# Attention with TensorE's order written out in steps, one unit ahead, and an eighth softmax tile

## The chip, the cores and the metric

The kernel runs on one core of a Trainium2 chip. The core has five engines that work side by side and meet at semaphores: TensorE (PE in the profile; its weight loads have a row of their own, PEld), VectorE (DVE), ScalarE (ACT), GpSimd (POOL) and SyncE (SP), which here only issues DMAs. The metric is the device time of one execution in microseconds (us). The kernel before took 1780.21 us, the median of three runs from 1777.09 to 1782.11 us.

## What is computed

The reference is a two-layer diffusion backbone over 1024 latent tokens and 256 context tokens, model width 1024. Layer 0 is gated attention, layer 1 a bidirectional state-space mixer (Mamba-2), and a last normalisation follows. The change is in layer 0, whose core is:

```python
q = axial_rope(q, row, col); k = axial_rope(k, row, col)
def block(j):                                   # 128 queries
    qb = q[:, j*128 : j*128+128]
    kb = concat(k_pad[3 blocks around j], k_c)  # up to 3 x 128 latent keys and 256 context keys
    s = einsum('bqkgd,bskd->bkgqs', qb, kb) * scale
    p = softmax over the keys and one sink logit per head, with a band mask
    return einsum('bkgqs,bskd->bqkgd', p, vb)
y_lat = (o * silu(g)) @ w_out
```

There are 16 query heads in 4 groups of 4; each group shares one key and value head of width 64. Context queries see the context keys alone. The projections of q, k, v and the gate g come from one input product, and `w_out` projects the gated result back; a residual with a gate and the normalisation of layer 1 follow.

## The kernel before, in words

Every product of 32-bit data is made of three matmuls of a reduced-precision type: high by high, high by low and low by high parts (`mm3`, lines 238 to 240, written to a PSUM tile `pj`). The parts are made by a copy on ACT and a subtraction on DVE or POOL.

The tokens are cut in three pieces: piece 0 and 1 are the latent tokens 0 to 511 and 512 to 1023, piece 2 the 256 context tokens. Before the stage that the change touches, the keys, the values, and queries and gates of pieces 0 and 2 have been projected; queries and gate factors lie in DRAM. The stage, `attention`, then works through 40 **units**. A unit is one block of 128 queries with one group of four heads: 8 units of context queries (blocks 8 and 9), 16 of piece 0 (blocks 0 to 3), 16 of piece 1 (blocks 4 to 7). A unit has 2 key blocks for context queries, 4 for the blocks at the edges (0 and 7) and 5 for the others.

What a unit does, with the lines of the code before:

- **front** (`att_front`): POOL issues the loads of the queries `qs` (L748) and of their zero-padded other half `qz` (L753), SP the load of the gate factors `sgt` (L749). For each of four heads TensorE makes the scores into a PSUM tile `S` (L767 latent keys, L768 context keys, each twice, for high and low query parts). DVE adds mask and scale and takes the row minimum (L772), into a softmax tile `sm`; ACT takes the exponential and its row sum (L774). Then the sums get the sink's share and are inverted and spread out (`rs`, L777 to L782).
- **back** (`att_back`): for each key block TensorE transposes the four heads' probabilities into one PSUM tile `pt` (L793); ACT copies it to a high part `ph` (L797), DVE subtracts to get the low part `pl` (L798), and two matmuls add the products with the values to the PSUM tile `pv` (L799 with `ph`, L800 with `pl`). At the end `rs` is transposed (L806) and multiplied into the gate factors (L807); ACT copies half of `pv` (`co`, L809), two DVE additions join the halves (`ot`, L812), POOL multiplies by the gate (L813), and ACT and POOL split the result (L815, L816).

PSUM has eight banks: two `S` tiles of two banks, two `pt`, one `pv`, one `pj`.

In between run **projection parts**: the remaining input projections (gates and queries of piece 1) during the first 24 units, then the output projections of pieces 2 and 0 during the last 16. A projection of 512 tokens is cut in eight parts of three matmuls (piece 2 in four parts of six). How many parts have been issued is paced by the count of key blocks done (`tick`). When a projection ends, its `pj` bank is read out: a gate by ACT and DVE (L661, L662), a query by four DVE and POOL steps and a split (L621 to L624, L642, L643), an output by one DVE step (L859) that adds the residual.

The order of the instructions on each engine is not that of the code. A planner sorts them by priority and by its own estimate of when each is ready. Code can tie an instruction behind another one of the same engine (`issue_after`) and raise a priority (`high_priority`). Before the change only the projection parts are tied, each behind the value product of some blocks back (`PACE`); all other work of TensorE in this stage is placed by the planner, one unit of fronts ahead (`AHEAD = 1`).

Of the kernel before, what the change touches and what calls it, by code (L numbers as in the profile page):

```python
# [9 lines left out]
F32 = mybir.dt.float32  # L10
BF16 = mybir.dt.bfloat16
F32R = mybir.dt.float32r
# [5 lines left out]
P = 128  # L18
D = 1024
# [24 lines left out]
    rope_b=2, qf=3, qh=3, ql=2, kHH=2, kLL=2, qs=2, sgt=2, sm=7, mx=2, nm=2, es=2, sums=2, ph=2, pl=2, co=1, ot=2,  # L44
# [4 lines left out]
AHEAD = 1  # L49
PACE = 4  # L50
# [5 lines left out]
FIRST = 5  # L56
# [57 lines left out]
class Kernel:  # L114
# [251 lines left out]
    def rstd_n(self, pool, pn, n, width, size=512, rout=None, dout=None, scalar=False):  # L366

        nc, t, ps = self.nc, self.t, self.psA
# [10 lines left out]
        pr = t(ps, [P, 512], F32, self.ptag)  # L379
# [360 lines left out]
    def att_front(self, p, x, i, j, b):  # L740
        nc, t = self.nc, self.t
        ps = self.psA
        o = b * P - TT[i][0]
        sg = t(self.psm, [P, 2, P], F32, "sgt")
        nm = t(p, [P, R], F32, "nm")
        sums = t(p, [P, R], F32, "sums")
        qs = t(p, [P, R, P], F32R, "qs")
        nc.gpsimd.dma_start(qs, self.q_d[j][i][:, :, :, o : o + P].rearrange("e s d n -> (s d) e n"))  # L748
        nc.sync.dma_start(sg, self.sg_d[j][i][:, :, o : o + P].rearrange("e p n -> p e n"))  # L749

        z = j % 2
        qz = self.qz[z]
        nc.gpsimd.dma_start(qz[z * HD : (z + 1) * HD], self.q_d[j][i][:, z, :, o : o + P].rearrange("e d n -> d e n"))  # L753
        if b < 8:
            k0, k1 = max(b - 1, 0), min(b + 2, 8)
        else:
            k0, k1 = 8, 8
# [5 lines left out]
        for r in range(R):  # L763
# [5 lines left out]
            self.scored.append(scored.ins)  # L769
# [5 lines left out]
            sms.append(sm)  # L775
        es = t(p, [P, R], F32, "es")
# [6 lines left out]
        return j, b, i, o, kb, sms, sg, rs  # L783

    def att_back(self, p, st, oH, oL, tick):
        nc, t = self.nc, self.t
        ps = self.psA
        j, b, i, o, kb, sms, sg, rs = st
        pv = t(ps, [P, 512], F32, "pv")
        for x, bb in enumerate(kb):  # L790
            pt = t(ps, [P, R, P], F32, "pt")
            for r in range(R):
                nc.tensor.transpose(pt[:, r, :], sms[r][:, x * P : (x + 1) * P], self.ident)  # L793
            ph = t(self.pb, [P, R * P], F32R, "ph")
            pl = t(self.pb, [P, R * P], F32R, "pl")
            ptf = pt.rearrange("p r n -> p (r n)")
            nc.scalar.copy(ph, ptf)  # L797
            nc.vector.tensor_sub(pl, ptf, ph)  # L798
            nc.tensor.matmul(pv, self.v[:, bb, j, :], ph, start=x == 0, stop=False)  # L799
            mm = nc.tensor.matmul(pv, self.v[:, bb, j, :], pl, start=False, stop=x == len(kb) - 1)  # L800
            self.last.append(mm.ins)
            tick()

        pt = t(ps, [P, 512], F32, "pt")
        for e in range(2):
            nc.tensor.transpose(pt[:, e * P : (e + 1) * P], rs[:, e].rearrange("p x d -> p (x d)"), self.ident)  # L806
        nc.vector.tensor_mul(sg, sg, pt[:, : 2 * P].rearrange("p (a n) -> p a n", a=2))  # L807
        co = t(self.pb, [HD, 512], F32, "co")
        nc.scalar.copy(co, pv[HD:, :])  # L809
        ot = t(self.pb, [P, 2, P], F32, "ot")  # L810
        for e in range(2):
            nc.vector.tensor_add(ot[e * HD : (e + 1) * HD].rearrange("p a n -> p (a n)"), pv[:HD, e * 256 : (e + 1) * 256], co[:, e * 256 : (e + 1) * 256])  # L812
        nc.gpsimd.tensor_tensor(ot, ot, sg, op=ALU.mult)  # L813
        oh = oH[i][:, 2 * j : 2 * j + 2, o : o + P]
        nc.scalar.copy(oh, ot)  # L815
        nc.gpsimd.tensor_tensor(oL[i][:, 2 * j : 2 * j + 2, o : o + P], ot, oh, op=ALU.subtract)  # L816

    def attention(self, c0, ckv):
# [7 lines left out]
        t(p, [P, 384], F32, "pad")  # L826
# [16 lines left out]
        def out_steps(i):  # L843
# [25 lines left out]
            def norm():  # L869
                p = self.po  # L870
                rout = (p, [P, n], F32, "ut" if i == 2 else "sqa")
                st["r"] = self.rstd_c(p, st["acc"], n, D, rout=rout, dout=(p, [P, 512], F32, "dg0"))
                self.alloc_u(i)

# [8 lines left out]
            def fin():  # L883
                yield
                for f in steps:
                    f()

            steps = [norm] + [lambda k=k: mod(k) for k in range(KT)]
# [11 lines left out]
        self.last = []  # L900
        cur = nxt = None

        def tick(flush=False):

            seen[i] += 1
            while done[i] < (total[i] if flush else min(total[i], -(-total[i] * seen[i] // count[i]))):
                advance(i, self.last[max(-len(self.last), -PACE)])

        def advance(i, after):
            nonlocal cur, nxt  # L910
            with self.tc.high_priority(offset=-300), self.tc.issue_after(after):
                if cur is None:
                    cur = nxt or fill[i].pop(0)()
                    if nxt is None:
                        next(cur)
                    nxt = None
                    if fill[i]:
                        nxt = fill[i].pop(0)()
                        next(nxt)
                if next(cur, "end") == "end":  # L920
                    cur = None
            done[i] += 1
            if i == 1 and self.side and done[i] > KT * CPARTS and (done[i] - KT * CPARTS) % SIDE == 0:
                self.side.pop(0)()

        self.scored = []
        pend = [self.att_front(p, x, *units[x]) for x in range(AHEAD)]
        for x in range(FIRST):
            advance(2, self.scored[1 if x < FIRST // 2 else 3])
        for x, (i, j, b) in enumerate(units):  # L930
            if oH[i] is None:
                if i == 1:
                    i = 0
                    tick(True)
# [6 lines left out]
            if x + AHEAD < len(units):  # L941
                pend.append(self.att_front(p, x + AHEAD, *units[x + AHEAD]))
            self.att_back(p, pend.pop(0), oH, oL, tick)
        tick(True)
# [871 lines left out]
```

## Time and profile before

| what | value |
|---|---|
| median of three runs | 1780.21 us (1777.09 to 1782.11) |
| the profiled execution | 1780.27 us |
| its span, first to last instruction | 1778.4 us |
| PE busy, weight loads busy | 98%, 85% of the span |
| DVE, ACT, POOL busy | 68%, 49%, 45% |
| attention stage, by its first score and its last block | about 244 to 687 us |

A row of groups reads: line, engine, operation, the tiles written and read, shapes, count, then the busy time in us and the mean ns of one, then the idle time of the engine just before them and what ended it. A timeline row gives start and length of an instruction or of several merged. The end of a matmul is modelled and lies some 0.16 us after the time at which the next one can start, so the distance from start to start is what a matmul costs, and "98% busy" does not say that the array is never waiting.

### The profile page before, as it was taken

The numbers are of one execution on the slowest core, as the hardware profiler recorded it, in microseconds if no ns is written. First come the engines' busy times: TensorE is split into PE (matmuls) and PEld (weight loads), VectorE is DVE, ScalarE is ACT, GpSimd is POOL, SyncE is SP. The second block draws the span as 40 slices with busy tenths as digits, with TensorE's granted clock in tenths as the row PEclk, the third lists the DMA queues.
The fourth block names the chain that finished last, engine by engine and source line by source line (L and its number), as shares of the span: only waits on it lengthen the run. The fifth ranks groups of instructions, "written<-read, shape, count | busy, mean of one in ns | idle before, by whom it ended". The sixth has DMA issues, their size and how long they took to land.

```text
span 1778.4 us, 29177 instructions
## 1 busy us (share of the span) xinstructions
PE 1739.9 (98%) x10413; PEld 1505.5 (85%) x10413; DVE 1204.2 (68%) x2119; ACT 871.8 (49%) x1902; POOL 796.8 (45%) x1066
## 2 busy tenths in 40 slices
PE   9999999999999999999999999999999999999997
PEld 6897788888888787778898898989889898988887
DVE  5744446788877875684876867677685767876634
ACT  4522247777777774352444444344443434544522
POOL 3231047555565545103454553636455363554321
PEclk9999999999999999999999999999999999999998
DMA  9478855444455446222323233332333333655533
GB/s 361 169 216 256 293 145 143 101 103 106 113 151 132 117 109 217 74 64 63 81 73 91 81 81 84 83 82 72 92 81 76 89 81 80 180 165 168 182 102 117
DMA packets 211388, 225.53 MB, mean 127 GB/s; under 512 B 15788, under 2 KB 149036, under 8 KB 211244
## 3 DMA queue, kind: packets, MB, share of 16 engines
q1 hardware_dynamic: 177180, 205.02, 39.0%
q0 software_dynamic: 34064, 18.65, 5.7%
q8 instruction: 82, 1.34, 0.3%
q14 instruction: 62, 0.51, 0.1%
HBM read 188.78 MB, written 35.13 MB: 126 GB/s over the span
## 4 chain that ended last, share of the span: by engine, by line
PE 84%; DVE 8%; DMA 2%; ACT 2%; issue 2%; POOL 1%; SPq 0%; DVEq 0%; ACTq 0%; POOLq 0%
PE pj L1213 18%; PE pj L1247 10%; PE pj L1648 7%; PE pj L238 6%; PE pj L239 6%; PE pj L240 6%; PE psD L1198 4%; PE psX L1400 3%; PE pt L793 3%; PE psD L1316 2%; PE pv L800 2%; PE psX L1369 2%; PE psX L1368 2%; PE pv L799 2%; PE S L767 1%
## 5 line engine op out<-in xcount | busy, mean ns | idle before, releaser
L238 PE MATMUL pj<-uH,wh 128*128 128x512 f32 (+1 forms) x680 | 244.1, 359 | 3.9 <-DVE h L859 2.0
L240 PE MATMUL pj<-uH,wl 128*128 128x512 f32 (+1 forms) x680 | 230.1, 339 | 1.4 <-POOL wl L223 1.4
L239 PE MATMUL pj<-uL,wh 128*128 128x512 f32 (+1 forms) x680 | 230.5, 339 | 0.4 <-POOL uL L816 0.4
L1213 PE MATMUL pj<-uH,wh 128*128 128x512 f32 x512 | 173.8, 411 | 1.2 <-ACT bn L1168 1.2
L1213 PE MATMUL pj<-uH,wl 128*128 128x512 f32 x512 | 170.4, 403 | 0.0
L1213 PE MATMUL pj<-uL,wh 128*128 128x512 f32 x512 | 168.2, 403 | 0.0
L1291 POOL TENSOR_TENSOR xw<-xn,dtdec 128x256 f32<-128x256 f32 x144 | 95.5, 664 | 160.4 <-PE psD L1316 75.8
L238 PEld LDWEIGHTS pj<-uH,wh 128*128 128x128 f32 x680 | 129.3, 190 | 28.0 <-ACT wh L221 5.7
L1247 PE MATMUL pj<-wh,uH 128*128 128x256 f32 x512 | 150.7, 294 | 0.0
L1247 PE MATMUL pj<-wl,uH 128*128 128x256 f32 x512 | 150.5, 294 | 0.0
L1247 PE MATMUL pj<-wh,uL 128*128 128x256 f32 x512 | 150.2, 293 | 0.0
L798 DVE TENSOR_TENSOR pl<-pt,ph 128x512 fp32r<-128x512 f32 x168 | 114.0, 688 | 47.2 <-ACT ph L797 46.2
L240 PEld LDWEIGHTS pj<-uH,wl 128*128 128x128 f32 x680 | 128.8, 190 | 17.3 <-POOL wl L223 2.2
L239 PEld LDWEIGHTS pj<-uL,wh 128*128 128x128 f32 x680 | 129.7, 191 | 10.5 <-issue 1.1
L223 POOL TENSOR_TENSOR wl<-wr,wh 128x512 fp32r<-128x512 f32 x74 | 97.2, 1316 | 84.7 <-ACT wh L221 83.8
L772 DVE CUSTOM_DVE_ANT_0 sm<-S,mask,nsink 128x640 f32<-128x640 f32 (+2 forms) x160 | 119.2, 772 | 20.6 <-PE S L768 13.5
L1432 ACT ACTIVATE uT<-psX,nw 128x128 f32<-128x128 f32 x128 | 46.5, 363 | 171.7 <-PE psX L1431 167.7
L774 ACT ACTIVATE sm<-sm,nm 128x640 f32<-128x640 f32 (+2 forms) x160 | 118.7, 742 | 17.5 <-DVE nm L772 16.9
L797 ACT CAST ph<-pt 128x512 fp32r<-128x512 f32 x168 | 97.4, 585 | 56.7 <-PE pt L793 52.4
L221 ACT CAST wh<-wr 128x512 fp32r<-128x512 f32 (+1 forms) x116 | 74.5, 648 | 81.8 <-PE pj L239 58.4
L1213 PEld LDWEIGHTS pj<-uH,wl 128*128 128x128 f32 x512 | 96.0, 188 | 19.9
L1213 PEld LDWEIGHTS pj<-uL,wh 128*128 128x128 f32 x512 | 95.5, 188 | 19.2
(352 smaller groups left out, 4945.3 us busy)
## 6 DMA issues: line engine op xcount, KB each, us to landing
wr<-w_x SPq DMA_DIRECT2D x32, 512.0 KB, 4.2
M<-acs SPq DMA_DIRECT2D x64, 256.0 KB, 5.3
bw<-acs SPq DMA_DIRECT2D x64, 256.0 KB, 5.6
wr<-w_sk SPq DMA_DIRECT2D x24, 512.0 KB, 4.1
wr<-wg SPq DMA_DIRECT2D x40, 256.0 KB, 5.2
qs<-q POOLq DMA_DIRECT2D x40, 256.0 KB, 3.9
wada<-w_ada SPq DMA_DIRECT2D x16, 512.0 KB, 8.6
wr<-wq SPq DMA_DIRECT2D x32, 256.0 KB, 3.1
```

Source lines behind the costliest of these rows:

```text
L223: (eng or nc.vector).tensor_tensor(l, raw, h, op=ALU.subtract)
L238: self.nc.tensor.matmul(ps, lh, rh, start=first and i == 0, stop=False)
L239: self.nc.tensor.matmul(ps, lh, rl, start=False, stop=False)
L240: self.last_mm = self.nc.tensor.matmul(ps, ll, rh, start=False, stop=last and i == n - 1)
L772: nc.vector.tensor_tensor_reduce(out=sm[:, :W], in0=Sv, in1=self.mask[:, m0 : m0 + W], scale=-SCALE, scalar=self.nsink[:, 4 * j + r : 4 * ...
L774: nc.scalar.activation(sm[:, :W], sm[:, :W], AF.Exp, bias=nm[:, r : r + 1], scale=-1.0, accum_out=sums[:, r : r + 1])
L797: nc.scalar.copy(ph, ptf)
L798: nc.vector.tensor_sub(pl, ptf, ph)
L1213: self.pe = nc.tensor.matmul(raw[:, 512 * i : 512 * i + 512], l[:, k, :], r[i][:, k, :], start=k + y == 0, stop=k == KT - 1 and y == 2)
L1247: self.pe = nc.tensor.matmul(pj[:, c], l, r[:, k, :], start=c % 2 + q + k + y == 0, stop=c % 2 == 1 and q == 1 and k == 3 and y == 2)
L1291: nc.gpsimd.tensor_tensor(xw, X(st, c).rearrange("p (r h) -> p r h", r=R), self.dtdec[:, c, hd(d, g)].unsqueeze(2).broadcast_to([P, R, HP] ...
L1648: self.pe = nc.tensor.matmul(banks[x], l[:, z, sl], r, start=k == 2 * qs[0] and y == 0, stop=k == 2 * qs[-1] + 1 and y == 2)
```

## The change

`att_front` becomes a generator that yields after each head, and `att_load` issues its two query loads one unit earlier, right after the first head of the unit before. `att_back` is split into `att_turn` (the four transposes of one key block, ACT's copy, DVE's subtraction), `att_gate` (the transposes of `rs` and the multiplication) and `att_out`. A helper `tied` puts every group of TensorE's instructions in this stage behind the last one before it, so TensorE's order is that of the code:

- five heads are done before the first unit's products begin;
- then for key block k of a unit: the transposes of block k+1; projection parts that end a projection; one head of a later unit's scores (`HEADS_AT`); at k = 0 the rest of the parts; the product with `ph`; at k > 0 the rest of the parts; at the last block the transposes of the next unit's block 0; the product with `pl`; parts that begin a projection; at the last block but one the gate's transposes.

`PARTS_AT` says at which block a unit's parts are put. There are eight softmax tiles `sm` in place of seven; `rs` has one buffer in place of two, and an unused tile of 384 words (`pad`) is gone. The normalisation behind the output projection of piece 2 is cut in two steps (`norm`, `factor`) that are issued six parts apart.

```diff
-sm=7
+sm=8
-AHEAD = 1
-PACE = 4
-FIRST = 5
+PARTS_AT = {5: (0, 0, 1, 2, 3, 4), 4: (0, 0, 1, 2, 3), 2: (0, 0, 1, 0, 1)}
+HEADS_AT = {5: ((1, 0), (1, 0), (1, 0), (0, 0), (1, 0)), 4: ((1, 0), (1, 0), (1, 0), (1, 0)), 2: ((2, 1), (1, 0))}
...
-        rs = t(self.pb, [P, 2, 2, HD], F32, "rs", 2)
+        rs = t(self.pb, [P, 2, 2, HD], F32, "rs")
...
+    def att_turn(self, sms, x):
+        nc, t = self.nc, self.t
+        pt = t(self.psA, [P, R, P], F32, "pt")
+        for r in range(R):
+            mm = nc.tensor.transpose(pt[:, r, :], sms[r][:, x * P : (x + 1) * P], self.ident)
+        ph = t(self.pb, [P, R * P], F32R, "ph")
+        pl = t(self.pb, [P, R * P], F32R, "pl")
+        ptf = pt.rearrange("p r n -> p (r n)")
+        nc.scalar.copy(ph, ptf)
+        nc.vector.tensor_sub(pl, ptf, ph)
+        return mm, (ph, pl)
...
-        t(p, [P, 384], F32, "pad")
...
+        def tied(f, *args):
+            nonlocal last
+            with ExitStack() as c:
+                if last:
+                    c.enter_context(self.tc.issue_after(last.ins))
+                out = f(*args)
+            mm = out[0] if isinstance(out, tuple) else out
+            last = mm or last
+            return out
...
+        def stream():
+            q = [self.att_load(p, 0, *units[0])]
+            for x, u in enumerate(units):
+                for r, mm in enumerate(self.att_front(p, q[x], x, *u)):
+                    if r == 0 and x + 1 < len(units):
+                        q.append(self.att_load(p, x + 1, *units[x + 1]))
+                    yield mm
...
+            for k, bb in enumerate(kb):
+                if k + 1 < n:
+                    _, w1 = tied(self.att_turn, sms, k + 1)
+                ends = [edge(i, d + y) for y in range(want[k])]
+                d += want[k]
+                early = max([y + 1 for y in range(want[k]) if 1 in ends[y]], default=0)
+                late = want[k] - early if early or want[k] and 0 in ends[0] and k else 0
+                advance(i, early)
+                heads(HEADS_AT[n][k][0])
+                if k == 0:
+                    advance(i, want[0] - early - late)
+                    pv = t(ps, [P, 512], F32, "pv")
+                vv = self.v[:, bb, j, :]
+                tied(nc.tensor.matmul, pv, vv, w[0], k == 0, False)
+                heads(HEADS_AT[n][k][1])
+                if k:
+                    advance(i, want[k] - early - late)
+                if k == n - 1 and self.pend:
+                    _, w1 = tied(self.att_turn, self.pend[0][1], 0)
+                tied(nc.tensor.matmul, pv, vv, w[1], False, k == n - 1)
+                advance(i, late)
+                if k == n - 2:
+                    tied(self.att_gate, sg, rs)
+                w = w1
```

More of the change, by code (lines that the diff above doesn't have):

```diff
@@ L786, in att_back @@
         nc, t = self.nc, self.t
[L787 to L802, printed above, removed]
@@ L886, in fin @@
                     f()
-            steps = [norm] + [lambda k=k: mod(k) for k in range(KT)]
+                self.last_mm = None
+            steps = [norm, factor] + [lambda k=k: mod(k) for k in range(KT)]
             if i == 2:
@@ L926, in attention @@
[L926 to L929, printed above, removed]
+        cur = nxt = last = None
+        self.pend = []
+        def tied(f, *args):
[7 more added lines that the diff above has]
+            return out
@@ new lines, in part, with advance @@
+        def part():
+            nonlocal cur, nxt
+            self.last_mm = None
+            if cur is None:
+                cur = nxt or fill[i].pop(0)()
+                if nxt is None:
+                    next(cur)
+                nxt = None
+                if fill[i]:
+                    nxt = fill[i].pop(0)()
+                    next(nxt)
+            if next(cur, "end") == "end":
+                cur = None
+            return self.last_mm
+        def advance(i, m):
+            for _ in range(m):
+                with self.tc.high_priority(offset=-300):
+                    tied(part)
+                done[i] += 1
+                if i == 1 and self.side and done[i] > KT * CPARTS and (done[i] - KT * CPARTS) % SIDE == 0:
+                    tied(self.side.pop(0))
@@ new lines, in heads, with gate @@
+        def heads(m):
+            for _ in range(m):
+                if tied(next, scores, None) is None:
+                    break
+        def gate(x):
+            i, j, b = units[x]
+            o = b * P - TT[i][0]
+            sg = t(self.psm, [P, 2, P], F32, "sgt")
+            nc.sync.dma_start(sg, self.sg_d[j][i][:, :, o : o + P].rearrange("e p n -> p e n"))
+            return sg
+        scores = stream()
+        i = 2
+        for m, f in ((2, 2), (2, 2), (1, 1)):
+            heads(m)
+            advance(2, f)
```

96 lines of the change are left out of this document (52 added, 44 removed).

## The prediction

> **What bounds the kernel now.** I read the page first, then the busy time by stretches, then TensorE's groups with their shapes, the timeline, and last the waits of TensorE's weight loads.
>
> ```profile
> PE 84%; DVE 8%; DMA 2%; ACT 2%; issue 2%; POOL 1%; SPq 0%; DVEq 0%; ACTq 0%; POOLq 0%
> ```
>
> The chain that ended last is TensorE for 84%, so the question is how much of the attention stage TensorE spends on something other than issuing matmuls. The stretches are the stage (244 to 687 us) and ten of its five-block units; after the length stand the busy times of PE, PEld, DVE, ACT and POOL with their counts, the granted clock, and the DMA share.
>
> ```profile
> 244.00:687.00 443.00, 430.20 (x2517) 364.91 (x2515) 328.71 (x732) 314.46 (x719) 255.55 (x365) 1.00 0.50 124
> 371.04:491.18 120.14, 117.40 (x676) 99.20 (x675) 101.55 (x209) 84.97 (x183) 68.64 (x93) 1.00 0.47 108
> ```
>
> The clock is full (1.00). No other engine is full on the whole: DVE 328.71 of 443.00 us (74%), ACT 71%. In the ten units, where query projections are read out, DVE is at 85%. What a matmul costs is the distance between starts.
>
> ```profile
> 303.73 0.60 PE L793 MATMUL pt<-ident,sm 128*128 128x128 f32 x4
> 304.09 0.36 PE L767 MATMUL S<-kHH,qs 128*128 128x256 f32 x1
> 304.29 0.28 PE L768 MATMUL S<-kHH,qs 128*128 128x256 f32 x1
> 304.41 0.28 PE L767 MATMUL S<-kL,qz 128*128 128x256 f32 x1
> ...
> 405.35 0.40 PE L238 MATMUL pj<-uH,wh 128*128 128x512 f32 x1
> 405.58 0.39 PE L239 MATMUL pj<-uL,wh 128*128 128x512 f32 x1
> ...
> 406.04 0.34 PE L767 MATMUL S<-kHH,qs 128*128 128x384 f32 x1
> 406.22 0.28 PE L768 MATMUL S<-kHH,qs 128*128 128x256 f32 x1
> ```
>
> A 512-wide matmul costs 0.23 us (405.35 to 405.58), a 384-wide one 0.18, a 256-wide one 0.12 (304.29 to 304.41). Four transposes cost 0.36, and the matmul behind them 0.20 in place of 0.12: 0.44 together, 0.11 each.
>
> ```profile
> L793 PE MATMUL pt<-ident,sm 128*128 128x128 f32 x672 | 99.8, 273 | 0.1
> L238 PE MATMUL pj<-uH,wh 128*128 128x512 f32 x204 | 90.6, 444 | 1.3 <-DVE qf L662 0.9 <-DVE h L859 0.4
> L800 PE MATMUL pv<-pl,v 128*128 128x512 f32 x168 | 69.6, 414 | 6.1 <-DVE pl L798 5.4
> L768 PE MATMUL S<-kHH,qs 128*128 128x256 f32 x160 | 45.9, 290 | 0.3 <-DVE nm L772 0.3
> L767 PE MATMUL S<-kHH,qs 128*128 128x384 f32 x96 | 34.9, 363 | 0.1
> L238 PE MATMUL pj<-uH,wh 128*128 128x256 f32 x64 | 19.5, 305 | 1.6 <-DVE h L859 1.6
> L806 PE MATMUL pt<-ident,rs 128*128 128x128 f32 x80 | 15.3, 272 | 0.1
> L767 PE MATMUL S<-kHH,qs 128*128 128x256 f32 x32 | 10.2, 319 | 0.7 <-DVE nm L772 0.7
> ```
>
> L239 and L240 stand beside L238, L799 beside L800, the `kL,qz` half beside each `kHH,qs` row, with the same counts. So 3 x 204 + 2 x 168 = 948 matmuls of 0.23 (218 us), 2 x (160 + 32) + 3 x 64 = 576 of 0.12 (69), 192 of 0.18 (35), 672 + 80 transposes of 0.11 (83): 405 us. With some 8 us for the first matmuls of the next stage that fall into the window (an estimate, about 35 at 0.23), the floor is 413 of 443 us. About 30 us are waiting. The waits of the weight loads show the same sum, and where it lies:
>
> ```profile
> PEld pv L800 <- DVE pl L798: 13.8, 25, 2.3
> PEld pv L799 <- ACT ph L797: 3.7, 8, 1.1
> PEld pj L238 <- DVE h L859: 2.9, 3, 1.9
> PEld S L767 <- DVE nm L772: 2.1, 4, 0.8
> PEld pj L238 <- DVE qf L662: 1.3, 2, 1.1
> ```
>
> These make 23.8; nine smaller rows bring it to about 28. Products that wait for their split probabilities are 17.5 of that, the `pj` bank 4.2, scores 2.1.
>
> **The change, part by part.** It computes the same matmuls, so the floor stays; only the roughly 28 us can move, and what the new order adds. I compare, for each wait, the work that the order puts in between (the cover) with the chain that must fit behind it. The pieces from the costs above: a block's transposes 0.44, one head (two of 0.18, two of 0.12) 0.60, a part of three 0.69, a product 0.23, the gate's transposes 0.22. A five-block unit is then 5 x (0.44 + 0.46) + 4 x 0.60 + 5.8 parts (88 parts over 76 blocks) x 0.69 + 0.22 = 11.1 us, against 120.14 / 10 = 12.0 now.
>
> The chains, from these rows (the timeline around one unit's end, then groups of DVE in the ten units, of ACT at 288 to 462 us, and POOL's longest wait):
>
> ```profile
> 407.28 0.40 PE L800 MATMUL pv<-pl,v 128*128 128x512 f32 x1
> 407.52 0.60 PE L793 MATMUL pt<-ident,sm 128*128 128x128 f32 x4
> 407.72 0.58 ACT L809 COPY co<-pv 64x512 f32<-64x512 f32 x1 [0.58 <-PE pv L800]
> 409.19 0.84 DVE L812 TENSOR_TENSOR ot<-pv,co 64x256 f32<-64x256 f32 x2
> 410.28 0.40 PE L799 MATMUL pv<-ph,v 128*128 128x512 f32 x1
> 410.67 1.28 DVE L798 TENSOR_TENSOR pl<-pt,ph 128x512 fp32r<-128x512 f32 x2
> 411.41 0.50 PE L800 MATMUL pv<-pl,v 128*128 128x512 f32 x1 [0.73 <-DVE pl L798]
> ```
>
> ```profile
> L772 DVE CUSTOM_DVE_ANT_0 sm<-S,mask,nsink 128x640 f32<-128x640 f32 x41 | 34.9, 878 | 2.2 <-PE S L768 1.5 <-PE pt L793 0.6
> L798 DVE TENSOR_TENSOR pl<-pt,ph 128x512 fp32r<-128x512 f32 x50 | 34.0, 688 | 14.2 <-ACT ph L797 13.9
> L643 DVE TENSOR_TENSOR ql<-qf,qh 128x512 fp32r<-128x512 f32 x7 | 8.1, 1154 | 0.2
> L622 DVE STREAM_SHUFFLE rope_b<-pj 128x512 f32<-128x512 f32 x8 | 5.9, 738 | 0.0
> ```
>
> ```profile
> L774 ACT ACTIVATE sm<-sm,nm 128x640 f32<-128x640 f32 x43 | 35.6, 828 | 4.7 <-DVE nm L772 4.3
> ```
>
> ```profile
> POOL qs L748 <- PE S L768: 39.7, 24, 11.0
> ```
>
> - *Products.* From the last transpose to `pl`: about 0.4 until ACT starts (407.28 to 407.72 for the copy `co`), 0.58 for the copy as for `co`, 0.69: 1.7 us with both queues empty. With one exponential (0.83) and one mask step (0.88) in front it is 3.4; in the unit above it was 3.9 (407.52 to 411.41), behind four heads in a row. The new order puts a product, a part, a product, transposes, a head, a product and a part between: 0.23 + 0.69 + 0.23 + 0.44 + 0.60 + 0.23 + 0.69 = 3.1 us, and a step without a part or a head some 0.6 less. With one head a step there is seldom more than one exponential and one mask step in front, so most chains fit and some are late by a few tenths. Bounds for the sum: 0, and 24 (a third of 168 late by 0.4). I take 6, a third of today's 17.5, nearer the empty-queue row because the heads come singly.
> - *The bank `pv`.* The next unit's first product waits until `co` and both additions have read it: 0.4 + 0.58 + 0.84 = 1.9 with empty queues; above it took 2.75 (407.28 to 410.03). Cover: product 0.23, transposes 0.44, head 0.60, two parts 1.38, in all 2.65. Today the planner fills this place with whatever is ready; now nothing else may go first. Bounds 0 and 30 (`co` behind an exponential and the additions behind a mask step: 1.9 + 0.83 + 0.88 = 3.6, 0.95 late in 32 units of four or five blocks). I take 5, about 0.15 per unit, near the observed 2.75.
> - *The bank `pj`.* The part that ends a projection goes to the front of its step, the one that begins the next to the end of the following one: head 0.60, two products 0.46, transposes 0.44, head 0.60, two products: 2.5 us. A query needs 0.4, the shuffle's 0.74 and a multiplication of about its length, 1.9, plus its turn in DVE's queue. From 4.2 to 2; bounds 0 and 32 edges x 0.5 = 16.
> - *Scores and softmax tiles.* One head a step: both earlier readers of an `S` tile have two steps (over 4 us) for 0.88 and less. The eighth tile lets the head of the unit after next start when the last transposes are done. From 2.1 to 0.5; bounds 0 and 2. The rest (the nine smaller rows, 4.5, normalisation and gate among them) goes to 3, as the cut in `norm` and `factor` puts six parts between DVE's diagonal and its matmul.
> - *Queues passed.* The two query loads now come a unit ahead, right behind the last reader of their buffers, so POOL's 39.7 us of waiting at L748 should nearly go. POOL is off the chain, so I count nothing; it covers late low weights (L223). If it were not gone, weight splits behind it would hold L240. With one `rs` buffer POOL's copy must wait for the gate's transposes at the last block but one; the sums of the next unit are ready at about that time (its last head is at the third block, 3 us before), so at most some tenths, with the next loads and weight splits behind it. SP's gate load waits for a tile freed two units before, as now; the weight loads and output stores behind it wait the same.
>
> Sum of waits after: 6 + 5 + 2 + 0.5 + 3 = 16.5 us, against 28.3: 12 us less. The profiled execution took 1780.27, its span 1778.4, so 1.9 lie outside and stay; it agrees with the median 1780.21. Forecast: 1780.2 - 12 = **1768 us**.
>
> The Trainium skill (Perfetto Trace Analysis, Identifying the Most-Contended Engine) takes the weight loads' busy share, not the matmuls', as TensorE's headroom. Here that is 364.91 of 443.00, so 78 us of room and 1702 us; the distances between starts bear out 30, as a 512-wide matmul takes 0.23 whatever its load takes, so that time gets no chance.
>
> **The rivals.**
>
> 1. *Nearly all waits go.* The covers hold everywhere. 1780 - 26 = 1754. For it: empty-queue chains of 1.7 and 1.9 fit with room; against: DVE at 10.2 us per 11.1 us unit leaves queues seldom empty.
> 2. *DVE takes over as the limit; no change.* In the ten units DVE is busy 101.55 / 10 = 10.2 us per unit and waits 1.4 more for `ph` (13.9 / 10). If that wait stays, a unit cannot be under 11.6: 0.4 gained in each of 24 five-block units, 10 us, and late `pv` additions in the same queue give back 5 to 8. 1776. For it: the split L643 takes 1154 ns against 688 for L798 of the same size, so DVE is slowed there already. The Trainium skill (SBUF, Who interferes with whom) has a DVE instruction with two SBUF inputs, as L643, block whole against GpSimd's reads, while L798 has one input in PSUM; the two rows agree, and a denser unit would hit more of it: at another 0.5 us per unit DVE, not TensorE, sets the pace by an estimate from these rows.
> 3. *The single `pv` bank; slower.* ACT serves `co` behind an exponential and DVE the additions behind a mask step in every unit of four or five blocks: 0.95 x 32 = 30 us in place of 5, so 1768 + 25 = 1793. It decides from about (5 + 12 + 5) / 32 = 0.7 us late per unit. For it: fixed order, ACT at 71% and the new unit's `ph` due at the same moment; against: 2.75 observed with 2.65 of cover.
>
> **How the numbers follow.** My forecast, with its sum between 1760 and 1774, has 0.46; rival 1 0.18; rival 2 0.18; rival 3 0.18. The point is the likeliest case. Fast ends with rival 1 (1754), slow with rival 3 at nearly its full price, so 1752 to 1790; alone, my case has 1760 to 1774. A change under 0.3% (5 us) can't be told from none. Faster are my case and rival 1: 0.64; rival 2 the same: 0.18; rival 3 slower: 0.18.
>
> **What the changed profile would show.** Right: the stage near 431 us; L800's wait for `pl` under 6 us; POOL's wait at L748's counterpart almost gone; mask steps one at a time, not four in a row. Wrong: first products of a unit (`pv` with `ph`) waiting for the additions `ot` by more than 0.7 us each; first parts of a projection waiting for `pj`; DVE over 95% busy in the query units; or a transpose that waits for the exponential of the next unit's last head.

## The result, and the profile after

The changed kernel takes 1799.76 us (median of five runs, 1797.82 to 1807.75) against 1778.40 us of the kernel before beside it: a ratio of 1.0123, with a 95% interval from 1.0098 to 1.0149. It is slower by about 21 us; the forecast was 12 us faster. The profiled execution took 1797.82 us with a span of 1796.1.

The page of the changed kernel: TensorE's busy share and the chain that ended last.

```profile
PE 1736.1 (97%) x10413; PEld 1503.8 (84%) x10413; DVE 1197.3 (67%) x2119; ACT 877.8 (49%) x1902; POOL 793.5 (44%) x1066
...
PE 84%; DVE 7%; issue 3%; ACT 3%; DMA 2%; POOL 1%; SPq 0%; DVEq 0%; ACTq 0%; POOLq 0%
```

Same work, more waiting. The attention stage, which was forecast at 431 us, takes 450 (columns as in the prediction):

```profile
244.00:694.00 450.00, 414.31 (x2455) 352.77 (x2454) 321.16 (x728) 315.39 (x712) 247.89 (x360) 0.99 0.46 116
```

DVE is busy 321.16 of 450.00 us (71%) and ACT 70%: neither has become the limit. The waits of TensorE in that stretch say what has (L920 is the line of `tied` from which both products with the values now come, L237 to L239 are the projection's three matmuls, L810 is the gate's transpose, L798 a block's):

```profile
PE pv L920 <- DVE ot L820: 18.6, 17, 2.2
PE pj L237 <- DVE h L865: 4.0, 1, 4.0
PE pj L237 <- DVE qf L668: 3.6, 6, 0.9
PE pt L810 <- POOL rs L790: 3.0, 3, 1.5
PE pv L920 <- ACT wh L220: 1.4, 2, 0.9
PE pv L920 <- ACT ut L872: 1.2, 1, 1.2
PE S L775 <- DVE nm L778: 1.0, 2, 0.6
```

The first row is the bank of value sums: a unit's first product waits for the additions that read the last unit's sums. Before, the same view for the same stretch began:

```profile
PE pv L800 <- DVE pl L798: 5.4, 12, 1.9
PE pj L238 <- DVE h L859: 2.0, 2, 1.6
PE pv L799 <- DVE ot L812: 1.6, 2, 0.9
```

These idle times begin only when the modelled end of the last matmul is past, so they are too short. For the comparison of runs I took the distance from each start to the next within the stage, less the cost of the matmul by the prediction (0.23, 0.18, 0.12, 0.11 us), and summed what is over 0.15 us by the matmul that comes next. In us:

| kernel | unit's first product | low-part products | parts | gate | transposes | scores | all |
|---|---|---|---|---|---|---|---|
| before | 2.6 | 10.0 | 3.7 | 0.3 | 0.2 | 1.9 | 20.3 |
| after | 25.4 | 1.2 | 9.6 | 4.5 | 2.3 | 2.1 | 45.1 |

The column "all" also has 1.6 us before of places that are not listed. So the waits for `pl` are nearly gone, 8.8 us gained, and 22.8 us are lost at first products, 5.9 at the projection bank, 4.2 at the gate. The smaller losses per matmul, which the table leaves out, fell by some 4 us. One place of the bank's wait, from the timeline of the changed kernel:

```profile
377.05 0.83 ACT L780 ACTIVATE sm<-sm,nm 128x640 f32<-128x640 f32 x1 [2.06 <-DVE nm L778]
377.19 0.48 PE L920 MATMUL pv<-pl,v 128*128 128x512 f32 x1
377.51 0.60 PE L798 MATMUL pt<-ident,sm 128*128 128x128 f32 x4
377.88 0.56 ACT L802 CAST ph<-pt 128x512 fp32r<-128x512 f32 x1
378.47 0.58 ACT L817 COPY co<-pv 64x512 f32<-64x512 f32 x1
...
379.08 0.68 DVE L627 TENSOR_TENSOR qf<-pj,cos 128x512 f32<-128x512 f32 x1
379.69 0.73 DVE L628 STREAM_SHUFFLE rope_b<-pj 128x512 f32<-128x512 f32 x1
380.31 0.83 DVE L820 TENSOR_TENSOR ot<-pv,co 64x256 f32<-64x256 f32 x2
381.28 0.47 PE L920 MATMUL pv<-ph,v 128*128 128x512 f32 x1 [1.88 <-DVE ot L820]
```

The unit's last product starts at 377.19. With ACT free, the copy `co` could follow 0.4 us later. Here an exponential holds ACT until 377.88, and then ACT casts `ph`, the next unit's block 0, whose transposes the new order puts in front of that product. The copy ends at 379.05, but DVE reads out a query before it comes to the additions at 380.31, so at this place DVE's turn costs more than the cast. The next unit's first product starts 4.1 us after the last one, and TensorE stands for about 2 of them with scores, transposes and parts behind it that it may not issue. Over the 40 units the copy starts 1.23 us after the start of the last product on the mean, before 0.74. From 0.4 us after that product's start to the copy, ACT spends 20.1 us in all on the next unit's cast, before 0.4. The additions end at 3.09 us on the mean, before at 2.60: the whole difference, 0.49 us, arises ahead of the copy.

The stage also gives up some filling: the planner used to put matmuls of the next stage among the last units' waits, and mostly no longer does. The first of those into `S` tiles, before and after:

```profile
L238 PE MATMUL S<-uH,wh x40: 388/390/487, 670.7 to 722.7; 128*128 128x512 f32 x40
```

```profile
L237 PE MATMUL S<-uH,wh x40: 389/389/798, 693.4 to 739.0; 128*128 128x512 f32 x40
```

From its first score to its last product the stage takes 433.0 us before and 446.7 after, 13.7 more, though it holds some 7 us less work by the costs of the matmuls (397 in place of 404). That work comes later, and what follows the stage takes 4.8 us more; what precedes it takes 0.8 less. Together these are the 17.7 us between the two profiled spans.

Some long waits are followed by a lower clock. The granted clock is 0.50 in two short stretches of the changed kernel's stage (columns as before):

```profile
382.20:385.60 3.40, 3.40 (x14) 2.90 (x13) 2.56 (x4) 2.33 (x5) 1.99 (x3) 0.50 0.41 116
511.90:515.30 3.40, 3.40 (x16) 3.12 (x15) 0.87 (x2) 1.16 (x2) 0.09 (x1) 0.50 0.56 129
```

They begin 0.9 and 0.7 us after waits of 2.0 and 4.2 us have ended (at 381.28 and 511.22), and in the first one a 512-wide matmul takes 0.43 us to the next start (382.37 to 382.80) in place of 0.23. Other waits of 2.0 and 2.4 us, which end at 465.7 and 621.7, are followed by none. The kernel before has no such stretch in its stage. As an estimate, at most half of the 6.8 us is lost, 3.4 us; about 1.5 us of it stands in the table, among parts, scores, gate and transposes. The five executions of the changed kernel have a mean granted clock of 0.990 to 0.995, 0.992 on the mean, and the profiled one has 0.995; the kernel before has 0.992 to 0.998 in all the sessions below, 0.996 on the mean. By these means (0.004 of 1798 us) up to some 7 us of the 21 would be lost as clock, again an estimate. No run separates this share from the waits that it comes with.

### The profile page after: what moved, and what is told of

Read it like the earlier page. It is cut to its first block, busy times and chain, and to the rows that moved or that the text cites. A ratio compares the mean times of both kernels' runs of the same rounds, so it can differ in the third digit from the quotient of the medians.

```text
span 1796.1 us, 29272 instructions
## 1 busy us (share of the span) xinstructions
PE 1736.1 (97%) x10413; PEld 1503.8 (84%) x10413; DVE 1197.3 (67%) x2119; ACT 877.8 (49%) x1902; POOL 793.5 (44%) x1066
## 4 chain that ended last, share of the span: by engine, by line
PE 84%; DVE 7%; issue 3%; ACT 3%; DMA 2%; POOL 1%; SPq 0%; DVEq 0%; ACTq 0%; POOLq 0%
PE pj L1296 18%; PE pj L1330 10%; PE pj L1731 7%; PE pj L237 6%; PE pj L238 6%; PE pj L239 6%; PE psD L1281 4%; PE pv L920 4%; PE psX L1483 3%; PE pt L798 3%; PE psD L1399 2%; PE S L774 2%; PE psX L1452 2%; PE psX L1451 2%; PE S L775 1%
## 5 line engine op out<-in xcount | busy, mean ns | idle before, releaser
L237 PE MATMUL pj<-uH,wh 128*128 128x512 f32 (+1 forms) x680 | 235.9, 347 | 7.9 <-DVE h L865 4.0
L239 PE MATMUL pj<-uH,wl 128*128 128x512 f32 (+1 forms) x680 | 229.8, 339 | 0.0
L237 PEld LDWEIGHTS pj<-uH,wh 128*128 128x128 f32 x680 | 129.5, 190 | 31.3 <-DVE qf L668 7.0
L778 DVE CUSTOM_DVE_ANT_0 sm<-S,mask,nsink 128x640 f32<-128x640 f32 (+2 forms) x160 | 123.0, 773 | 40.2 <-PE S L775 39.1
L239 PEld LDWEIGHTS pj<-uH,wl 128*128 128x128 f32 x680 | 129.0, 190 | 15.4 <-issue 0.8
L238 PEld LDWEIGHTS pj<-uL,wh 128*128 128x128 f32 x680 | 129.5, 190 | 13.3 <-issue 1.1
```

The lines of the kernel that those rows point to most:

```text
L237: self.nc.tensor.matmul(ps, lh, rh, start=first and i == 0, stop=False)
L238: self.nc.tensor.matmul(ps, lh, rl, start=False, stop=False)
L239: self.last_mm = self.nc.tensor.matmul(ps, ll, rh, start=False, stop=last and i == n - 1)
L778: nc.vector.tensor_tensor_reduce(out=sm[:, :W], in0=Sv, in1=self.mask[:, m0 : m0 + W], scale=-SCALE, scalar=self.nsink[:, 4 * j + r : 4 * ...
```

## The experiments

The theories at the start. **A**: the one bank of value sums costs, since ACT serves the next unit's cast first and TensorE may not go on. **B**: the tile changes cost (one `rs` buffer, eight `sm`). **C**: a written-out order waits some 40 us in any case, and only the place changes. Ratios are to the kernel before in the same session; differences in us between runs are of medians from sessions in which the kernel before took 1776.1 to 1778.4. The waits named are those of the table's method.

### The transposes behind the last product

```diff
-                if k == n - 1 and self.pend:
-                    _, w1 = tied(self.att_turn, self.pend[0][1], 0)
                 tied(nc.tensor.matmul, pv, vv, w[1], False, k == n - 1)
+                if k == n - 1 and self.pend:
+                    _, w1 = tied(self.att_turn, self.pend[0][1], 0)
```

> The changed kernel, but the next unit's first transposes come right behind a unit's last product instead of in front of it, so that ScalarE is asked for the copy out of the value bank before it is asked for the next unit's cast (0.58 us). Theory A (the one bank of value sums stands empty-handed because ScalarE casts first and TensorE may not go on to other work): the waits of first products for that bank, about 25 us over the stage by the distances between starts, fall by about 0.5 us in each of 39 units to some 8 us, and the time falls by 10 to 18 us, to 1782 to 1790. Theory B (the tile changes: one rs buffer, eight softmax tiles): within 3 us of the changed kernel's 1800. Theory C (a written-out order always waits somewhere, the wait only changes its place): the bank's waits fall but others rise, 1795 to 1800.

1797.66 us, ratio 1.0094 (1.0063 to 1.0125): 2 us less than the changed kernel, inside the spread of either. The first products' waits fall from 25.4 to 4.0, and the low-part products' rise from 1.2 to 20.0; its waits begin:

```profile
PE pv L920 <- DVE pl L803: 14.2, 22, 1.4
PE pj L237 <- DVE h L865: 5.3, 1, 5.3
```

A's chain is right, since the cast did stand ahead of the copy; its price is not, since whichever of the two ACT does first, the other is late for a product that comes next. (17.0 us of this run's stage are at the granted clock of 0.50.) This speaks for C, or for a shortage of other work at that one place.

### Two banks for the value sums and for the projections, one score tile

```diff
-            BUFS.update(S=2, pj=1)
+            BUFS.update(S=1, pj=2, pv=2)
...
-                yield from self.proj_g(out, ps, w, oH, oL, i, "S" if i == 1 and m % 3 else "pj", parts={0: PARTS, 1: 1, 2: CPARTS}[i])
+                yield from self.proj_g(out, ps, w, oH, oL, i, "S" if i == 1 and m % 3 == 1 else "pj", parts={0: PARTS, 1: 1, 2: CPARTS}[i])
...
-HEADS_AT = {5: ((1, 0), (1, 0), (1, 0), (0, 0), (1, 0)), 4: ((1, 0), (1, 0), (1, 0), (1, 0)), 2: ((2, 1), (1, 0))}
+HEADS_AT = {5: ((1, 0), (1, 0), (1, 0), (0, 0), (1, 0)), 4: ((1, 0), (1, 0), (1, 0), (1, 0)), 2: ((1, 1), (1, 1))}
```

> The changed kernel with two banks for the value sums and two for the projections, paid for with one score tile in place of two; context units do their heads one by one. Theory A: the waits at the value bank (25 us) and at the projection bank (8 us) go, and the single score tile costs some, since a head's mask step (0.9 us) must end before the next head (2 us later): 1765 to 1780. Theory B: about 1800. Theory C: the waits move to the scores, 1790 or more.

1796.34 us, 1.0087 (1.0054 to 1.0121). First products wait 0.2 us, parts 0.9, and scores 26.4 in place of 2.1:

```profile
PE S L774 <- DVE nm L778: 12.1, 17, 1.7
PE S L775 <- DVE nm L778: 6.8, 11, 1.6
```

With a second bank the turn of the unit costs next to nothing, and the single score tile costs nearly as much. In this fixed order, then, this split of the eight banks only moves the wait. The Trainium skill (Perfetto Trace Analysis, Optimization Strategy) says that the same gap coming back on the engine that should be full can mean that PSUM or SBUF is too short for the next tile. The traces agree: the 25.4 us come back at the same place in 22 of 39 turns and go with the second bank (a later run ends them without one, by untying two products).

### Only the parts tied

```diff
-                if last:
-                    c.enter_context(self.tc.issue_after(last.ins))
+                if prods and f == part:
+                    c.enter_context(self.tc.issue_after(prods[max(-len(prods), -8)].ins))
...
+            if f == nc.tensor.matmul and not args[-2]:
+                prods.append(out)
```

> The changed kernel with its code order, its tiles and its early loads, but only the projection parts tied (behind a product some blocks back); the planner places everything else on TensorE, as before the change. Theory A: TensorE can again fill the place in front of a unit's first product, 1775 to 1785. Theory B: stays at 1795 or more, for tiles and loads are those of the changed kernel. Theory C: like A, 1775 to 1785; it is told from A by the other two runs.

1784.75 us, 1.0028 (1.0011 to 1.0046). Two thirds of the loss go with the ties, with tiles, loads and the order of the code unchanged. 7 us stay, now as first products (9.3) and transposes (8.4) that wait. B falls as the main cause.

### The tile changes alone

```diff
-sm=7
+sm=8
...
-        rs = t(self.pb, [P, 2, 2, HD], F32, "rs", 2)
+        rs = t(self.pb, [P, 2, 2, HD], F32, "rs")
...
-        t(p, [P, 384], F32, "pad")
```

> The kernel before with only the tile changes: eight softmax tiles, one rs buffer, no unused tile. Theory A and C: no change, 1776 to 1783. Theory B: 1790 or more.

1774.76 us, 0.9973 (0.9955 to 0.9991): on the kernel before, the tiles are a small gain. B, a loss by the tiles, is out.

### One part less, or more, at the turn of the unit

**D** replaces A: ACT and DVE owe TensorE some 3.1 to 3.5 us at the turn, and the fixed order has 2.65 us of other work there.

```diff
-PARTS_AT = {5: (0, 0, 1, 2, 3, 4), 4: (0, 0, 1, 2, 3), 2: (0, 0, 1, 0, 1)}
+PARTS_AT = {5: (0, 1, 2, 3, 3, 4), 4: (0, 1, 2, 3, 3), 2: (0, 0, 1, 0, 1)}
```

> The changed kernel with one projection part (0.69 us) moved from block 0 of each unit of four or five blocks to a later block, so less independent work stands between a unit's last product and the next unit's first. Theory D (at the turn of a unit ScalarE and VectorE owe TensorE some 3.1 to 3.5 us of work, and the fixed order gives 2.65 us of other work to cover it, while the other places have cover to spare): first products wait about 0.5 to 0.69 us more in 32 units, 16 to 22 us, so 1813 to 1820. Theory C (a fixed order waits about 40 us in any case, only the place changes): within 5 us of 1798.

```diff
-PARTS_AT = {5: (0, 0, 1, 2, 3, 4), 4: (0, 0, 1, 2, 3), 2: (0, 0, 1, 0, 1)}
+PARTS_AT = {5: (0, 0, 0, 1, 2, 3), 4: (0, 0, 0, 1, 2), 2: (0, 0, 1, 0, 1)}
```

> The opposite step: one more part at block 0, none at the last block, in units of four or five blocks. Theory D: first products wait about 0.4 us less in 32 units, 12 us, a few of it given back at the last blocks: 1786 to 1791. Theory C: 1795 to 1800.

The first took 1819.34 us, 1.0247 (1.0229 to 1.0265); the second 1794.78, 1.0108 (1.009 to 1.0127). First products wait 39.4, 25.4 and 7.9 us with one part less, as changed, and one more: the dose works. The gain does not: of 17.5 us at first products, 5 reach the time. Parts now wait 16.9 us in place of 9.6 (mostly for the steps that read out the projection's single bank; 6.4 of them are one late load, shown below), and transposes 5.0 in place of 2.3. The stretches at half the granted clock go the same way as the waits: 20.4 us of the stage with one part less, 6.8 as changed, and by half of these 13.6 us, an estimate, up to 7 of the 20 us that the first run loses on the changed kernel are clock. D for the loss, C for the repair.

### Two heads in front as well, and the gate of context units later

```diff
-PARTS_AT = {5: (0, 0, 1, 2, 3, 4), 4: (0, 0, 1, 2, 3), 2: (0, 0, 1, 0, 1)}
+PARTS_AT = {5: (0, 0, 0, 1, 2, 3), 4: (0, 0, 0, 1, 2), 2: (0, 0, 1, 0, 1)}
-HEADS_AT = {5: ((1, 0), (1, 0), (1, 0), (0, 0), (1, 0)), 4: ((1, 0), (1, 0), (1, 0), (1, 0)), 2: ((2, 1), (1, 0))}
+HEADS_AT = {5: ((2, 0), (1, 0), (0, 0), (0, 0), (1, 0)), 4: ((2, 0), (1, 0), (0, 0), (1, 0)), 2: ((2, 1), (1, 0))}
...
-                if k == n - 2:
+                if k == max(n - 2, 1):
                     tied(self.att_gate, sg, rs)
```

> As the run before, and also two heads' scores (0.60 us more) in front of a unit's first product and none at the third block, and for context units the gate's transposes at the last block, a step later. Theory D: the first products' waits all but end (25 us to under 5), the gate's 4.5 us too: 1775 to 1783 if the bunched heads cost nothing, a little more if mask steps now stand in the way of subtractions. Theory C: 1793 or more.

1797.86 us, 1.0115 (1.0095 to 1.0135): a miss. First products wait 5.5 us and the gate 0.2, as expected, but transposes 10.7 and parts 13.3.

### One more part, and the transposes behind the last product

This is the first edit together with one more part at block 0 and the later gate.

> One more part at block 0, the gate of context units a step later, and the next unit's first transposes behind the last product, as in the run in which the waits moved from first products (25.4 to 4.0 us) to low-part products (1.2 to 20.0 us). Theory D: those 20 us fall by 12 to 15, for the same 0.69 us stand in front of them: 1780 to 1786. Theory C: 1793 or more.

1800.57 us, 1.0137 (1.0114 to 1.0159): a miss too. Low-part products fall from 20.0 to 5.5 us, and transposes take 11.6, parts 15.0. In these runs, moving work to the front inside the fixed order handed most of the wait on.

### The copy out of the bank left out, in both kernels

`co0` is a tile of zeros, so both kernels leave the low half of the values out of their result.

```diff
-        co = t(self.pb, [HD, 512], F32, "co")
-        nc.scalar.copy(co, pv[HD:, :])
+        co = self.co0
```

> The changed kernel without ScalarE's copy out of the value bank: the additions take a tile of zeros in its place, so the low half of the values is left out of the result. The bank is then free after VectorE's two additions alone, and no other work is moved. Theory D (the turn of the unit is what costs): first products' waits fall from 25 us to under 5 and nothing takes their place, 1776 to 1784. Theory C (the waits go to the next place, as when parts were moved to the front): 1790 or more.

> The same copy left out of the kernel before, whose low half of the values is then missing as well. Its first products wait 2.6 us in all, so by theory D it gains 1 to 5 us: 1772 to 1776. If the copy's own 0.58 us on ScalarE mattered whatever the order, it would gain as much as the changed kernel does, 15 us.

The changed kernel takes 1780.32 us, 1.0014 (1.0002 to 1.0026), 19 us less. The kernel before takes 1771.75, 0.9967 (0.9954 to 0.998), 6 us less. First products wait 0.8 us in the one, 2.3 in the other. The waits that are left in the changed kernel begin:

```profile
PE pj L237 <- DVE h L866: 5.5, 3, 5.2
PE pj L237 <- DVE qf L668: 4.0, 5, 1.7
```

Here nothing was moved, only the chain shortened. Of the 24.6 us gone at first products some 5 come back elsewhere (parts rise by about 4 us and low-part products by 3, the gate falls by 2). The same 0.58 us per unit is worth some 14 us more under the fixed order than under the planner's. That is D's share of the 21 us by this test, which also takes 23 us of work off ACT in both kernels.

### Seven softmax tiles and two buffers of `rs`

> The changed kernel with seven softmax tiles and two rs buffers, as before the change. If the eighth tile is what the written-out order lives on, the head of the unit after next now waits for tiles and the time rises by 5 us or more; if the single rs buffer is behind the gate's 4.5 us of waits, these go and the time falls by up to 4 us. Theory D expects 1795 to 1803.

1803.51 us, 1.0132 (1.0108 to 1.0156): by the intervals not to be told from the changed kernel. By the medians the eighth tile is worth 4 us at most, and the gate's waits (3.1 us, 4.5 with one buffer) are only in small part the single buffer.

### The tiles and the cut normalisation, with the planner's order

> The kernel before with the tile changes and the normalisation cut in two steps, its order still the planner's. The tiles alone gave a ratio of 0.9973 to the kernel before; the cut takes away up to 1 us of waiting at the diagonal's matmul: 1771 to 1776, faster than both kernels by a little.

1774.09 us, 0.9979 (0.9967 to 0.999). This, or the tiles alone, beats the kernel before by 0.2 to 0.3%, and the changed kernel by some 1.4%.

### The first two products of a unit off the chain

```diff
-                tied(nc.tensor.matmul, pv, vv, w[0], k == 0, False)
+                (nc.tensor.matmul if k == 0 else lambda *z: tied(nc.tensor.matmul, *z))(pv, vv, w[0], k == 0, False)
```

and the same for the product with the low part.

> The changed kernel with only the two products of each unit's block 0 left out of the written-out chain; everything else stays tied in its order, and the planner may let the next block's transposes and a head pass these two. Theory D, in its form that TensorE may not pass the waiting product: the 25 us of first products' waits fall to 5 to 12 us and the time to 1784 to 1792. If it is not the tie but the late bank itself that costs (the work behind runs dry as well), 1796 to 1800.

1784.52 us, 1.0029 (1.0016 to 1.0042), 15 us under the changed kernel. First products wait 1.9 us, though parts now wait 17.5. In 30 of 39 turns the planner puts one more block's transposes and one more head in front of these two products. The additions end 3.06 us after the last product on the mean, as late as in the changed kernel (3.09). Thus the bank is late in any case, and it is the tie that makes its lateness cost. What is left begins with

```profile
PE pj L237 <- DVE h L865: 6.8, 5, 5.4
PE pj L237 <- DVE qf L668: 4.6, 6, 1.1
```

### A tile of its own for the first residual block

Every run with the full tie and one projection bank has one wait of 4 to 6 us. In the changed kernel:

```profile
507.58 0.91 SPq L861 DMA_DIRECT2D h<-ctxT  x2
...
510.68 0.48 DVE L865 SCALAR_TENSOR_TENSOR h<-pj,mod,h 128x256 f32<-128x256 f32 x1 [2.50 <-DMA h<-ctxT]
511.22 0.39 PE L237 MATMUL pj<-uH,wh 128*128 128x256 f32 x1 [3.97 <-DVE h L865]
```

The first output projection is done, its bank waits for the residual, and the residual's load is issued only then. With seven `sm` tiles and one `rs` buffer there is room for a tile outside the memory that the query projections still hold:

```diff
-                h1 = t(self.o1, [P, n], F32, "h1k") if i == 1 else t(p, [P, n], F32, "h1")
+                h1 = t(self.o1, [P, n], F32, "h1k") if i == 1 else t(*((self.ph1, [P, n], F32, "h1c") if i == 2 and m == 0 else (p, [P, n], F32, "h1")))
```

> Seven softmax tiles, one rs buffer, and in the room a tile of its own for the first residual block of the first output projection, so that its load need not wait for the query projections' memory. The one wait of 4 to 6 us for the projection bank at the start of the output projections goes: 4 to 6 us under the run with seven tiles (1803.5), so 1796 to 1800. If that wait is for something else, no change.

1796.27 us, 1.01 (1.0085 to 1.0115): 7 us under the run with seven tiles, whose interval just overlaps this one, and 3.5 under the changed kernel. So the time alone puts the gain at some 4 to 7 us. In the trace it is plain: the wait is gone, with the 6.8 us at half the granted clock that stood beside it in the run with seven tiles (from 513.5), and parts wait 5.1 us in place of 12.4:

```profile
PE pv L921 <- DVE ot L820: 18.8, 15, 2.1
PE pj L237 <- DVE qf L668: 2.7, 5, 0.9
```

### Both repairs, on the changed kernel, and the load's on the kernel before

In the first, the gate of context units also comes a block later.

> Both repairs at once on the changed kernel (a unit's first two products off the chain; seven softmax tiles and a tile of its own for the first residual block), and the gate of context units a block later. If the two places found are the whole loss, the single gains add up: 1800 less 15, less 7, less some of the gate's 4: 1775 to 1780, level with the kernel before. If they overlap or another wait takes their place, 1784 or more.

> The kernel before with one rs buffer, the normalisation cut in two, seven softmax tiles and the same tile for the first residual block. There the planner filled most of that wait with other work (1.9 us were left), so 0 to 3 us under the kernel before: 1774 to 1778.

The first takes 1779.63 us, 1.0008 (0.9994 to 1.0022), level with the kernel before: the products off the chain give 15 us, and the load's tile and the later gate another 5. The stage has no stretch at half the granted clock any more, and first products wait 1.3 us; transposes (10.6) and parts (10.7) are what waits now. The second takes 1779.24, 1.0006 (0.9995 to 1.0016): no gain. In the kernel before, the wait at that place is only 1.8 us (at 499.5), filled by the planner with other work.

## Why the prediction was wrong

- *What bounds the stage.* Right: the matmuls are the same and the loss is all waiting. DVE did not become the limit (71% of the stage), so rival 2 fell, and rival 1 with the waits that came.
- *Products.* Right, and better than taken: low-part products wait 1.2 us, down from 10.0; I had taken 6 for both parts. (A third of 168 late by 0.4 is 22, not the 24 of my upper bound; the sum does not use it.) Heads come one at a time: DVE's mask steps wait for scores in 57 places, 39.1 us, before 21 and 13.5.
- *The bank `pv`.* This is the step that failed. I took 5 us and the runs show 25.4. My waits after summed to 16.5, the table's to 45.1, and this one term is 20.4 of the 28.6 between; with 5 here the change would have come out about level (24.7 against 20.3 before, and the smaller losses 4 lower), so the other terms missed the gain as well. The cover of 2.65 us was about right in the units with two parts ahead of the first product. The chain was mis-sized: I let `co` start after 0.4 us as in the row quoted, and counted the next unit's transposes as cover, but not that they put a cast into ACT's queue ahead of `co`. It ended at 3.09 us on the mean. And where a projection ends in block 0, the part that begins the next goes behind the product, so the cover is one part less (1.96 us); three of the four longest waits, 1.9 to 2.1 us, are there. Rival 3 had the place, the price (0.95 per unit, 1793) and the point of decision (0.7 late per unit; measured 25.4 / 32 = 0.8). It named an exponential and a mask step ahead; ACT gave the cast, which it did not name, 20.1 us and exponentials 11.6, so it was nearly right in size and only in part in cause. I gave it 0.18 because the observed 2.75 us lay so near the cover. The mean of a chain near its cover is no zero; only the late half counts under a tie.
- *The bank `pj`.* Mis-sized: 2 taken, 9.6 measured, 4.2 of them the one late residual load. I had the load's row in neither the chain nor the queues. The planner had hidden it behind other work; the tie did not.
- *Scores, gate, rest.* Taken 3.5, measured 2.1 + 4.5 + 2.3. The gate of context units comes too early for `rs`: a block later it waits 0.2 us or less.
- *Queues passed.* Wrong: POOL still waits 44.7 us at the query loads (39.7 before). They still stand in POOL's queue ahead of the end of the scores that free their buffer, though the code issues them a unit earlier. No run tests whether this costs anything:

```profile
POOL qs L750 <- PE S L775: 44.7, 25, 14.9
```

- *The clock.* I read it as full (1.00) and let a wait cost its own length. In the changed kernel two stretches of 3.4 us at 0.50 follow long waits, an estimated 3.4 us more at most in the profiled execution.
- *The base.* I compared each place's cover with a chain and took the rest of the order as neutral. Runs with work moved to the front show what was left out: cover at one place is taken from another. The table's sum falls from 45.1 us to 36.8, 36.5 and 34.5 with one part, with heads as well, and with the transposes behind, and the time only by 5 us, by 2, and not at all.

Shown by runs: the turn of the unit under the tie (15 us, by letting other work pass) and the late residual load (4 to 7 us). Open: how much of each is the waits themselves and how much the granted clock that falls beside them; why 7 us stay when all ties but the parts' are gone, with first products and transposes waiting in another mixture, and why the last shifts' 8 to 11 us of shorter waits hardly reach the time; more of the next stage's matmuls then lie inside the stage (11 us by their costs), but what follows is not shorter by as much (8.6 us with one part more).

## What to carry to other kernels

In this kernel an order written out by hand made a late buffer cost its full lateness, where the planner's order had some other work to put there; so before writing it out, list for each single buffer the engine that frees it and what that engine has been given just ahead, including by the transposes or copies that the new order itself moves up. Let the one or two instructions that wait for such a buffer off the chain: that gave back 15 of 21 us here, more than any shift of work inside the chain. And when a repair moves the wait rather than ending it, shorten the chain instead of moving work, as a test: leaving out the 0.58 us copy told in one run what five shifts did not.

## What the runs showed that was not expected

A copy of 0.58 us per unit on ScalarE was worth 19 us in 40 units under the fixed order (0.49 per unit) and 6 under the planner's. A second bank for value sums and projections took away 33.9 us of waits (25.4 + 9.6, less the 0.2 and 0.9 left), and one score tile less cost 24.3 at the scores (26.4 - 2.1); the time fell by only 3 us. And the granted clock follows the waits: the stage has 6.8 us at 0.50 in the changed kernel, 20.4 with one part less at the turn, and none in the kernel before or with both repairs.
